# A hybrid decoder layer on one core: two instead of three of eight k-pairs by seven products, token sums formed with the tokens, and two of four weight sums formed by accumulating DMAs

## The chip, the cores and the metric

The kernel runs on one core of a Trainium2 chip. A time is the device time of one execution in microseconds (us). The kernel before takes 2048.77 us, the median of three runs (2047.95 to 2048.99). TensorE (PE) multiplies, VectorE (DVE) and ScalarE (ACT) do the elementwise work, SyncE (SP) issues loads and DMA transposes, GpSimd (POOL) does a few small operations.

## The reference

One decoder layer over 256 tokens of width 2048, in float32: a retention mixer and a gated linear recurrence side by side, merged by sigmoid gates, then cross-attention to 256 memory tokens, then a gated FFN. Nearly all of the time is products of the 256 tokens with weight matrices:

```python
ret_out = jax.nn.silu(g_ret) * ret
rnn_out = jax.nn.gelu(yr) * hr
merged = (jax.nn.sigmoid(g_a) * (ret_out @ w_proj_ret[l])
          + jax.nn.sigmoid(g_b) * (rnn_out @ w_proj_rnn[l]))
h = h + merged @ w_mix_out[l]
...
h = h + memory_cross_attention(hn, mem_n, xa_w_q[l], xa_w_k[l], xa_w_v[l], xa_w_o[l])
...
h = h + conv_gated_ffn(hn, ffn_w_up[l], ffn_conv_w[l], ffn_conv_b[l], ffn_w_down[l])
```

`g_a` and `g_b` are column ranges of `hn @ w_in`.

## The kernel before

**Three products for one.** Every float32 operand is split into a high part, rounded to float32r, and a low part, the rest. A product of two blocks is then three matmuls: high by high, low by high, high by low. ACT copies the high part of a weight (lines 326 and 339), DVE subtracts it to get the low part (328 and 340). The stationary operand is a 128 x 128 block of tokens, the moving one a 128 x 512 block of weights.

**Chunks.** `weight_plan` lists the matrix products in order, and `weights_in_order` lays all weights out in the order of their use, in chunks of 1 MB: 128 partitions x 4 blocks x 512 columns. `prefetch` loads a chunk into one of three `raw` buffers and splits it into `hi` and `lo` tiles (`PART_BUFS = 6` tiles of two blocks each); it keeps two chunks ahead of PE. `gemm_n` multiplies by one column block of 512; its chunk is four k-tiles, 24 matmuls.

**Pairs.** `steps_pair` multiplies by two column blocks at once. Its chunk is one k-pair (two k-tiles of 128) by both column blocks, and there are eight k-pairs to 2048 inputs. An ordinary k-pair takes 8 block products, 24 matmuls. A k-pair listed in `SEVEN` takes seven block products instead (Winograd's form of Strassen's scheme over two token tiles, two k-tiles and two column blocks), 21 matmuls. For it, `seven_parts` forms four sums of weight blocks on DVE (line 349) and splits seven blocks, and `sums_of` forms four sums of token blocks (lines 428 to 438: tiles `g`, `tq`, and `ts` for the split sums). `sums_of` is called from `steps_pair` one or two chunks ahead of the k-pair. The seven products are taken in the order p1, x3, p2, x5, p7, p6, p4; x3 is the first that reads `ts` and goes to a PSUM tile `sm`, so the profile shows it as `sm<-hi,ts`.

**Order of the stages.** Projections of `w_in` come first, then these pairs of column blocks, two per matrix: `w_proj_rnn`, gate columns `O_GA`, `w_proj_ret`, `w_mix_out`. A pair's eight chunks take some 41 us. After `w_proj_ret` the gates are applied (lines 934 and 956) and the rows are transposed by DMA (`by_dma`: ACT copies to `pl`, SP transposes into `pt`, ACT joins into `f`), and `turn_merged` splits them into the tokens of `w_mix_out`. Then come cross-attention (its `xa_w_o` has one pair, with `SEVEN_O`), and the FFN, whose first two `ffn_w_down` groups are two pairs each.

**Queues.** Each engine runs its instructions in the order in which they were recorded and scheduled; a waiting instruction holds what stands behind it. All loads and transposes stand in SP's one queue. At the start of `w_mix_out`, 4 MB of `x` and `mem` rows (tiles `nat`) are loaded through it too.

Of the kernel before, what the change touches and what calls it, by code (L numbers as in the profile page):

```python
# [17 lines left out]
P = 128  # L18
# [14 lines left out]
PART_BUFS = 6  # L33
# [8 lines left out]
SEVEN = (1, 3, 5)  # L42
# [25 lines left out]
def weight_plan():  # L68
# [81 lines left out]
def hybrid_layer(  # L150
# [106 lines left out]
    def prefetch(n):  # L257
        while len(ahead) < n and taken[0] < len(stream):
# [33 lines left out]
            own = early and i % 2 == 0  # L292
            cuts = () if i == 0 else range(0, nk + 1, KH) if i < 6 else (0, nk)
# [18 lines left out]
            if isinstance(c, tuple) and c[2]:  # L312
                ahead.append(((row, c), seven_parts(raw)))
                continue
            parts = []
            for k in range(0, nk, KH):
                if own:
                    xs[k2 + k // KH]
                hi = wp.tile([P, KH, BW], F32R, tag="hi", bufs=PART_BUFS, name=nm("hi"))
                lo = wp.tile([P, KH, BW], F32R, tag="lo", bufs=PART_BUFS, name=nm("lo"))  # L320
                for cs in (slice(k, k + 1), slice(k + 1, k + 2)) if i < 4 else (slice(k, k + KH),):
                    ds = slice(cs.start - k, cs.stop - k)
                    if i == 0 and cs.start == 0:
                        dve.tensor_copy(hi[:, ds], raw[:, cs, :])
                    else:
                        act.copy(hi[:, ds], raw[:, cs, :])  # L326
                    with tc.issue_after(split[cs.start]) if i == 0 else nullcontext():
                        dve.tensor_tensor(  # L328
                            out=lo[:, ds], in0=raw[:, cs, :], in1=hi[:, ds].bitcast(F32), op=ALU.subtract
                        )  # L330
                parts.append((hi, lo))
            ahead.append(((row, c), parts))

    def weight_parts(src):

        n = src.shape[1]
        hi = wp.tile([P, KH, BW], F32R, tag="hi", bufs=PART_BUFS, name=nm("hi"))
        lo = wp.tile([P, KH, BW], F32R, tag="lo", bufs=PART_BUFS, name=nm("lo"))
        act.copy(hi[:, 0:n], src)  # L339
        dve.tensor_tensor(out=lo[:, 0:n], in0=src, in1=hi[:, 0:n].bitcast(F32), op=ALU.subtract)  # L340
        return [(hi[:, i, :], lo[:, i, :]) for i in range(n)]

    def seven_parts(raw):

        b12, b11, b22, b21 = (raw[:, i, :] for i in range(4))
        p1, p3 = weight_parts(raw[:, 1:3])
        (p2,) = weight_parts(raw[:, 3:4])
        for o, a, b in ((b11, b12, b11), (b12, b12, b22), (b22, b11, b22), (b21, b22, b21)):
            dve.tensor_tensor(out=o, in0=a, in1=b, op=ALU.add)  # L349
# [42 lines left out]
    def steps_n(w, row, st, nk, col):  # L392
# [3 lines left out]
        for k0, n, parts in chunks(nk, w, row, col):  # L396

            def tile_(tt, kk):
                k = k0 + kk
                hi, lo = (t[:, kk % KH, :] for t in parts[kk // KH])  # L400
# [20 lines left out]
    def sums_of(t):  # L421

        if id(t) not in token_sums:
            g = big([P, 2, 2, P], s="g")
            o = big([P, 2, 4, P], F32R, s="ts")
            s = tmp("tq").rearrange("p a (b n) -> p (a b) n", b=2)
            flat = g.rearrange("p j i n -> p j (i n)")
            dve.tensor_tensor(
                out=flat, in0=t[:, :, 0:S].bitcast(F32), in1=t[:, :, S:BW].bitcast(F32), op=ALU.add
            )  # L430
            (a11, a21), (a12, a22) = ([g[:, j, i, :] for i in range(2)] for j in range(2))
            for d, a, b, op in (
                (0, a21, a22, ALU.subtract), (2, a11, a21, ALU.subtract),
                (1, s[:, 0, :], a11, ALU.subtract), (3, a12, s[:, 1, :], ALU.add),
            ):
                dve.tensor_tensor(out=s[:, d, :], in0=a, in1=b, op=op)
            act.copy(o[:, 0], s)  # L437
            dve.tensor_tensor(out=o[:, 1], in0=s, in1=o[:, 0].bitcast(F32), op=ALU.subtract)
            token_sums[id(t)] = (t, o)
        return token_sums[id(t)][1]  # L440

    def steps_pair(w, row, st, nk, c1, c2, seven=SEVEN):
# [14 lines left out]
        for k0, n, parts in chunks(nk, w, row, (c1, c2, seven)):  # L457
            k2 = k0 // KH
            for i in seven:
                if k2 < i <= k2 + 2:  # L460
                    sums_of(st[i])
# [5 lines left out]
            if k2 in seven:  # L467
# [5 lines left out]
                s1, s2, s3, s4 = ((ts[:, 0, i, :], ts[:, 1, i, :]) for i in range(4))  # L473
# [14 lines left out]
            else:  # L488
                end = k0 + n == nk
                for b, names in enumerate((("p2", "p4"), ("x3", "n"))):  # L490
                    hi, lo = parts[b]
# [219 lines left out]
    def split_head(h):  # L711
        f = words[h // 2][:, 2 * (h % 2) : 2 * (h % 2) + 2, :]
        ret.append(split_cols(f, lambda j: half_gn[:, 2 * h + j : 2 * h + j + 1]))

# [165 lines left out]
    for b in range(4):  # L880
# [28 lines left out]
        def gelu_y(f, xr=xr):  # L909
# [8 lines left out]
            for pr in range(2):  # L918
# [3 lines left out]
                rnn.append(split_pair(o, 0.5))  # L922
# [41 lines left out]
    def residual(w, st, out, wcol, steps=None):  # L964
# [3 lines left out]
        for b in range(4):  # L968
            if steps:
                steps(b)  # L970
            if not sources:
                if b == 0 or steps:
                    sources += pair(w, 0, st, NT, b * BW, (b + 1) * BW, *(() if steps else (SEVEN_O,)))
# [70 lines left out]
    def split_block(f):  # L1044
        return [split_pair(f[:, 2 * pr : 2 * pr + 2, :]) for pr in range(2)]
# [213 lines left out]
```

## Time and profile before

| what | number |
|---|---|
| median of three runs | 2048.77 us |
| the profiled execution's own time | 2047.84 us |
| its span, first to last instruction | 2046.1 us |
| mean granted TensorE clock | 0.987 |
| PE busy | 1991.3 us (97%), 8840 matmuls |
| DVE busy | 1542.0 us (75%) |
| ACT busy | 1343.0 us (66%) |
| POOL busy | 25.3 us (1%) |
| DMA | 425.60 MB, 208 GB/s mean |

The span is 1.7 us under the execution's time. Busy times are averages over stages with different limits: the pairs are read apart from the rest below. A matmul's duration in the rows (389 ns) overlaps with the next one's, so pace is read from counts in a stretch, not from durations.

### The profile page before, as it was taken

How to read it: one execution, taken by the hardware profiler on the slowest of the kernel's cores; microseconds unless marked ns; L12 is line 12 of the kernel's file. 1: busy time of each engine (PE TensorE's matmuls, PEld its weight loads, DVE VectorE, ACT ScalarE, POOL GpSimd, SP SyncE). 2: the span in 40 equal slices, each digit the busy share in tenths (PEclk: the TensorE clock that was granted, in tenths of full speed). 3: DMA queues.
4: the chain of work that ended last, by engine and by line, in shares of the span. 5: the costliest groups of instructions: out<-in, count | busy, mean ns of one | idle time of the engine just before them, and what ended most of it. 6: DMA issues, size and time to landing. Idle time of an engine off the chain costs nothing.

```text
span 2046.1 us, 23900 instructions
## 1 busy us (share of the span) xinstructions
PE 1991.3 (97%) x8840; PEld 1643.7 (80%) x8840; DVE 1542.0 (75%) x2029; ACT 1343.0 (66%) x1615; POOL 25.3 (1%) x25
## 2 busy tenths in 40 slices
PE   9999999999999999699999999999989999899998
PEld 8888888888887877577888888888877888788887
DVE  6857766998699999787555568666789676897675
ACT  7647548988454656678666667777765567654773
POOL 0000001000000000000000000000000000000000
PEclk9999999999999999799999999999999999999999
DMA  8755656665555556567766656767655677556773
GB/s 324 249 198 183 227 185 208 205 234 196 185 193 191 190 212 202 199 205 242 228 203 206 208 185 216 227 197 224 226 157 197 211 215 226 187 183 220 226 226 124
DMA packets 197188, 425.60 MB, mean 208 GB/s; under 512 B 142032, under 2 KB 146640, under 8 KB 152016
## 3 DMA queue, kind: packets, MB, share of 16 engines
q1 hardware_dynamic: 197072, 424.09, 62.8%
q8 instruction: 69, 1.13, 0.2%
q14 instruction: 47, 0.39, 0.1%
HBM read 388.39 MB, written 2.10 MB: 191 GB/s over the span
## 4 chain that ended last, share of the span: by engine, by line
PE 80%; DVE 9%; ACT 5%; issue 3%; DMA 2%; POOL 0%; POOLq 0%; SPq 0%; DVEq 0%; ACTq 0%
PE acc L235 72%; PE sm L235 8%; DVE lo L340 3%; DVE raw L349 2%; DVE lo L328 2%; ACT hi L326 1%; ACT f L533 1%; ACT hi L339 1%; DMA pt<-pl 1%; DMA raw<-in_wall 1%; ACT pl L520 1%; ACT s L579 0%; DMA nat<-in_mem 0%; DVE s L580 0%; DVE fv L1090 0%
## 5 line engine op out<-in xcount | busy, mean ns | idle before, releaser
L235 PE MATMUL acc<-hi,s 128*128 128x512 f32 (+1 forms) x4812 | 1481.4, 389 | 1.8 <-ACT hi L326 0.8
L235 PEld LDWEIGHTS acc<-hi,s 128*128 128x128 f32 x4812 | 903.3, 188 | 189.3 <-ACT s L579 1.5
L328 DVE TENSOR_TENSOR lo<-raw,hi 128x1024 fp32r<-128x1024 f32 (+1 forms) x640 | 770.8, 1224 | 358.0 <-ACT hi L326 349.4
L235 PE MATMUL acc<-lo,s 128*128 128x512 f32 (+1 forms) x2406 | 935.8, 389 | 2.4 <-DVE lo L340 1.8
L326 ACT CAST hi<-raw 128x1024 fp32r<-128x1024 f32 (+1 forms) x639 | 651.0, 1044 | 270.4 <-PE acc L235 189.5
L235 PEld LDWEIGHTS acc<-lo,s 128*128 128x128 f32 x2406 | 453.3, 188 | 97.9 <-DVE lo L340 3.2
L339 ACT CAST hi<-raw 128x1024 fp32r<-128x1024 f32 (+1 forms) x152 | 140.9, 942 | 166.5 <-DVE raw L349 111.5
L533 ACT COPY f<-pt 128x1024 uint16<-128x1024 uint16 x128 | 168.4, 1353 | 74.7 <-DMA pt<-pl 74.6
L340 DVE TENSOR_TENSOR lo<-raw,hi 128x1024 fp32r<-128x1024 f32 (+1 forms) x152 | 162.5, 1087 | 26.7 <-ACT hi L339 25.4
L235 PE MATMUL sm<-hi,s 128*128 128x512 f32 x528 | 162.6, 389 | 0.6 <-ACT hi L326 0.6
L520 ACT COPY pl<-rows 128x1024 uint16<-128x1024 uint16 x100 | 99.6, 1043 | 53.2 <-DVE rows L546 40.2
L235 PEld LDWEIGHTS sm<-hi,s 128*128 128x128 f32 x528 | 99.0, 188 | 21.4 <-ACT hi L326 1.0
L349 DVE TENSOR_TENSOR raw<-raw 128x512 f32<-128x512 f32 x152 | 104.4, 687 | 1.5
L235 PE MATMUL sm<-lo,s 128*128 128x512 f32 x264 | 102.8, 389 | 0.5 <-DVE lo L328 0.5
L235 PE MATMUL acc<-hi,ts 128*128 128x512 f32 x228 | 77.2, 423 | 3.5 <-ACT hi L339 3.4
L235 PE MATMUL sm<-hi,ts 128*128 128x512 f32 x76 | 28.6, 441 | 34.8 <-ACT ts L437 29.4
L235 PEld LDWEIGHTS acc<-hi,ts 128*128 128x128 f32 x228 | 47.0, 208 | 15.2 <-ACT hi L339 4.9
L235 PEld LDWEIGHTS sm<-lo,s 128*128 128x128 f32 x264 | 49.6, 188 | 11.3 <-DVE lo L328 1.0
L546 DVE TENSOR_SCALAR rows<-acc,ro 128x512 f32<-128x512 f32 x76 | 53.3, 744 | 4.2 <-PE acc L235 4.2
L1090 DVE SCALAR_TENSOR_TENSOR fg<-f,pf,fg 128x255 f32<-128x255 f32 (+1 forms) x88 | 37.6, 478 | 22.3 <-ACT fg L1088 22.0
L235 PEld LDWEIGHTS sm<-hi,ts 128*128 128x128 f32 x76 | 15.0, 197 | 43.4 <-ACT ts L437 32.3
L235 PE MATMUL acc<-lo,ts 128*128 128x512 f32 x114 | 47.5, 417 | 2.1 <-DVE lo L340 2.1
(179 smaller groups left out, 1008.6 us busy)
## 6 DMA issues: line engine op xcount, KB each, us to landing
raw<-in_wall SPq DMA_DIRECT2D x352, 1024.0 KB, 4.8
nat<-in_x SPq DMA_DIRECT2D x8, 512.0 KB, 9.3
raw<-in_wall SPq DMA_DIRECT2D x7, 512.0 KB, 5.7
pt<-pl SPq DMA_TRANSPOSE x128, 3.2
nat<-in_mem SPq DMA_DIRECT2D x4, 512.0 KB, 9.7
xt<-in_x_t SPq DMA_DIRECT2D x3, 512.0 KB, 9.1
xt<-in_mem_t SPq DMA_DIRECT2D x3, 512.0 KB, 7.0
dec<-in_consts SPq DMA_DIRECT2D x2, 512.0 KB, 4.3
```

Of the source, the lines that this page charges most:

```text
L235: tc.keep_in_program_order(pe.matmul(*a, **k))
L326: act.copy(hi[:, ds], raw[:, cs, :])
L328: dve.tensor_tensor(out=lo[:, ds], in0=raw[:, cs, :], in1=hi[:, ds].bitcast(F32), op=ALU.subtract)
L339: act.copy(hi[:, 0:n], src)
L340: dve.tensor_tensor(out=lo[:, 0:n], in0=src, in1=hi[:, 0:n].bitcast(F32), op=ALU.subtract)
L349: dve.tensor_tensor(out=o, in0=a, in1=b, op=ALU.add)
L520: act.copy(planes[:, tt], words[:, tt])
L533: act.copy(halves_[:, :, :, cs], turned_[:, :, :, cs])
L546: dve.tensor_scalar_mul(rows[:, tt, :], a[:, tt, :], r[:, tt : tt + 1])
L1090: dve.scalar_tensor_tensor(out=y[:, s:S], in0=z[:, j, 0 : S - s], scalar=pf[:, 2 - s, t : t + 1], in1=y[:, s:S], op0=ALU.mult, op1=ALU.add,)
```

## The change

- **Which k-pairs.** `SEVEN` goes from (1, 3, 5) to (2, 5); `SEVEN_O` stays (3, 5). The second half of `w_mix_out` becomes two ordinary column blocks, one after the other. Chunks by seven products go from 38 to 24.
- **Weight sums.** A seven chunk is no longer one load. SP loads its fourth block twice into `raw[:, 0:2]` (a broadcast read), its first block into a tile `b11` of the `tmp` pool, and its middle blocks into `raw[:, 2:4]`. Then GpSimd issues a DMA that adds blocks 0 and 1 from HBM onto `raw[:, 0:2]`. That forms two of the four sums; DVE forms the other two from them.
- **Part tiles.** `PART_BUFS = 6` tiles of two blocks become 3 tiles of four blocks. An ordinary chunk of a pair is split by one ACT copy and one DVE subtraction of 2048 columns instead of two of 1024; chunks of `gemm_n` keep two of each. A seven chunk takes two tiles.
- **Token sums.** `with_sums` forms the sums right after the split of the tokens that need them, from the unsplit source, with three DVE sums instead of five. For `w_in` and `ret` tokens the source is still added up first; `ret` sums are formed in `split_head`, `O_GA` sums up to three chunks ahead.

```diff
-PART_BUFS = 6
+PART_BUFS = 3
...
-SEVEN = (1, 3, 5)
+SEVEN = (2, 5)
 SEVEN_O = (3, 5)
...
-    for w, c in (("w_proj_rnn", 0), ("w_in", O_GA), ("w_proj_ret", 0), ("w_mix_out", 0)):
+    for w, c in (("w_proj_rnn", 0), ("w_in", O_GA), ("w_proj_ret", 0)):
         plan += [(w, 0, NT, (c + b * BW, c + (b + 1) * BW, SEVEN)) for b in (0, 2)]
+    plan += [("w_mix_out", 0, NT, (0, BW, SEVEN))] + [("w_mix_out", 0, NT, b * BW) for b in (2, 3)]
...
-        order = (b[:, 0], a[:, 0], b[:, 1], a[:, 1]) if c[2] else (a[:, 0], a[:, 1], b[:, 0], b[:, 1])
+        order = (a[:, 0], b[:, 1], a[:, 1], b[:, 0]) if c[2] else (a[:, 0], a[:, 1], b[:, 0], b[:, 1])
...
+            if seven:
+                b11 = tmp("b11").rearrange("p a n -> p (a n)")
+                load(raw[:, 0:2], src[:, 3:4, :].to_broadcast([P, KH, BW]), False)
+                load(b11, src[:, 0, :], False)
+                load(raw[:, 2:4], src[:, 1:3, :], False)
+                pool.dma_start(out=raw[:, 0:2], in_=src[:, 0:2, :], accum_op=ALU.add)
+                ahead.append(((row, c), seven_parts(raw, b11)))
+                continue
...
-        b12, b11, b22, b21 = (raw[:, i, :] for i in range(4))
-        p1, p3 = weight_parts(raw[:, 1:3])
-        (p2,) = weight_parts(raw[:, 3:4])
-        for o, a, b in ((b11, b12, b11), (b12, b12, b22), (b22, b11, b22), (b21, b22, b21)):
-            dve.tensor_tensor(out=o, in0=a, in1=b, op=ALU.add)
-        q3, q1 = weight_parts(raw[:, 0:2])
-        q2, q4 = weight_parts(raw[:, 2:4])
+        t1, t3, b22, b21 = (raw[:, i, :] for i in range(4))
+        p_hi, p_lo = part_tiles()
+        q_hi, q_lo = part_tiles()
+        weight_parts(b11, p_hi[:, 0, :], p_lo[:, 0, :])
+        weight_parts(raw[:, 2:4], p_hi[:, 1:3], p_lo[:, 1:3])
+        dve.tensor_tensor(out=b22, in0=t1, in1=b22, op=ALU.add)
+        dve.tensor_tensor(out=b21, in0=b22, in1=b21, op=ALU.add)
+        for c in (slice(0, 2), slice(2, 4)):
+            weight_parts(raw[:, c], q_hi[:, c], q_lo[:, c])
...
+    def with_sums(out, seven, src, scale=None):
+
+        t = split_pair(src, scale)
+        if len(out) in seven:
+            sums_of(t, src, scale)
+        out.append(t)
...
-                if k2 < i <= k2 + 2:
+                if k2 < i <= k2 + 3 and (not isinstance(st, list) or i < len(st)):
                     sums_of(st[i])
...
-            merged.append(split_pair(f[:, 2 * pr : 2 * pr + 2, :], 0.5))
+            with_sums(merged, SEVEN, f[:, 2 * pr : 2 * pr + 2, :], 0.5)
```

`rnn`, `osp` and `hid` tokens get `with_sums` in the same way as `merged`.

Three places show what moves. The first is DVE at the passage from the second pair of `w_proj_ret` to the first pair of `w_mix_out`; `raw_6650` is a seven chunk, L934 and L956 apply the gates, L328 splits an ordinary chunk, `g`, `tq` and `ts` are token sums. Before:

```order
L349 TENSOR_TENSOR raw_6650<-raw_6650 128x512
L934 TENSOR_SCALAR o_6610<-o_5912,o_6610 128x1024
L340 TENSOR_TENSOR lo_6669<-raw_6650,hi_6668 128x1024
L956 TENSOR_TENSOR o_6610<-o_6610,o_5206 128x1024
L328 TENSOR_TENSOR lo_6740<-raw_6737,hi_6739 128x1024
L328 TENSOR_TENSOR lo_6744<-raw_6737,hi_6743 128x1024
L428 TENSOR_TENSOR g_6747<-s_6455 128x512
L436 TENSOR_TENSOR tq_6749<-g_6747 128x128 x2
L436 TENSOR_TENSOR tq_6749<-tq_6749,g_6747 128x128
L436 TENSOR_TENSOR tq_6749<-g_6747,tq_6749 128x128
L428 TENSOR_TENSOR g_6804<-s_6464 128x512
L438 TENSOR_TENSOR ts_6748<-tq_6749,ts_6748 128x512
```

The same passage after the change; `raw_6274` is the first seven chunk of `w_mix_out`, `b_902_6275` its tile `b11`, and L980 applies a gate:

```order
L980 TENSOR_TENSOR o_6167<-o_6167,o_4928 128x1024
L347 TENSOR_TENSOR lo_6281<-b_902_6275,hi_6280 128x512
L347 TENSOR_TENSOR lo_6281<-raw_6274,hi_6280 128x1024
L356 TENSOR_TENSOR raw_6274<-raw_6274 128x512
L357 TENSOR_TENSOR raw_6274<-raw_6274 128x512
L347 TENSOR_TENSOR lo_6283<-raw_6274,hi_6282 128x1024 x2
L347 TENSOR_TENSOR lo_6322<-raw_6319,hi_6321 128x2048
L347 TENSOR_TENSOR lo_6369<-raw_6366,hi_6368 128x2048
L443 TENSOR_TENSOR tq_6359<-f_6349 128x256
```

The token sums of the first seven chunk no longer stand behind the gates (they were formed in the pair ahead), two weight sums stand where four stood, and the ordinary chunks behind are split by one row of 2048 columns each. `tq_6359` belongs to the second seven chunk of this pair.

The second place is SP's queue in the same passage, after the change (`raw_6274` as above, `raw_6405` and `b_924_6406` of the second seven chunk):

```order
L207 DMA raw_6274<-in_wall 128x2x512
L207 DMA raw_6274<-in_wall 128x1024
L207 DMA raw_6319<-in_wall 128x2048
L207 DMA raw_6366<-in_wall 128x2048
L543 DMA_TRANSPOSE pt_6240<-pl_6239 128x8x128 x2
...
L203 DMA nat_6259<-in_x 128x2x512
L207 DMA nat_6261<-in_mem 128x1024
...
L207 DMA nat_6267<-in_mem 128x1024
L207 DMA raw_6405<-in_wall 128x2x512
L207 DMA b_924_6406<-in_wall 128x512
L207 DMA raw_6405<-in_wall 128x1024
```

Where one load of 128x2048 stood for a seven chunk there are now three (that of `b11` may stand far ahead of the others), and those of the second seven chunk stand behind the eight `nat` loads, as its one load did before.

The third place is POOL from its last copies for the recurrence to the root of the memory norm, after the change:

```order
L867 TENSOR_TENSOR rp_3584<-rgw_3418,rp_3583 128x1024
L300 DMA raw_4443<-in_wall 128x1024
L300 DMA raw_4546<-in_wall 128x1024
...
L300 DMA raw_6274<-in_wall 128x1024
L300 DMA raw_6405<-in_wall 128x1024
L647 TENSOR_TENSOR ro_6484<-rv_6482,mhalf 128x2
```

Before, L842/L843 and L625 stood next to each other there. Fourteen accumulating DMAs now stand between them (ten more follow in later stages), each behind a wait for the broadcast load of its chunk.

More of the change, by code (lines that the diff above doesn't have):

```diff
@@ L311, in prefetch @@
                     sum_squares(xin[b], ss0, b)
[L312 to L315, printed above, removed]
+            hi, lo = part_tiles()
             for k in range(0, nk, KH):
@@ L330, in prefetch @@
                         )
[L331 to L341, printed above, removed]
@@ L1207, in hybrid_layer @@
             vl = big([P, 4, S], s="fv")
-            conv_up(FF, b, vl, lambda b=b, vl=vl: gate_up(gts[b], vl, hid.setdefault(b, [])))
+            b0 = max(one[1] for one in ff_plan() if one[0] == "down" and one[1] <= b)
+            seven = tuple(i - 2 * (b - b0) for i in SEVEN) if b0 < sum(FF_PARTS[:2]) else ()
+            conv_up(FF, b, vl, lambda b=b, vl=vl, n=seven: gate_up(gts[b], vl, hid.setdefault(b, []), n))
         else:
```

93 lines of the change are left out of this document (56 added, 37 removed).

## The prediction

> **What bounds the kernel now.** The page comes first: PE is busy 97% of the span.
>
> ```profile
> PE 1991.3 (97%) x8840; PEld 1643.7 (80%) x8840; DVE 1542.0 (75%) x2029; ACT 1343.0 (66%) x1615; POOL 25.3 (1%) x25
> ```
>
> That is an average. The chain of work that ended last, taken over the gate-and-value stage of the FFN, shows PE's undisturbed pace: 976 matmuls in 221.06 us, 0.2265 us each.
>
> ```profile
> 1263.12 221.06 PE acc L235 x976
> ```
>
> With that pace I read the busy time by stretches, one stretch for each pair of column blocks and one for the start of each `ffn_w_down` group. Behind the length stand PE's busy time and, in brackets, its matmuls; the last three columns are granted clock, DMA share and GB/s.
>
> ```profile
> 557.50:598.00 40.50, 40.50 (x181) 33.53 (x180) 39.93 (x58) 22.81 (x26) 0.00 (x0) 1.00 0.56 208
> 598.00:646.00 48.00, 45.86 (x203) 37.65 (x201) 45.87 (x52) 23.93 (x26) 0.00 (x0) 1.00 0.52 192
> 646.00:690.00 44.00, 42.25 (x178) 34.63 (x179) 41.38 (x64) 29.44 (x44) 0.00 (x0) 0.96 0.48 173
> 732.00:778.00 46.00, 44.08 (x193) 35.97 (x192) 44.17 (x60) 24.62 (x28) 0.00 (x0) 1.00 0.55 198
> 778.00:822.00 44.00, 41.38 (x178) 32.65 (x176) 39.92 (x48) 29.18 (x34) 0.00 (x0) 1.00 0.63 200
> 822.00:882.00 60.00, 44.47 (x152) 33.06 (x151) 44.58 (x64) 35.60 (x45) 0.70 (x1) 0.80 0.65 223
> 882.00:944.00 62.00, 57.57 (x239) 45.77 (x237) 52.19 (x67) 47.86 (x69) 0.00 (x0) 0.94 0.66 212
> 1496.00:1560.00 64.00, 55.47 (x234) 44.59 (x233) 62.39 (x95) 38.04 (x46) 0.00 (x0) 0.95 0.46 156
> 1762.00:1830.00 68.00, 61.45 (x257) 49.67 (x256) 66.16 (x98) 41.03 (x51) 0.00 (x0) 0.95 0.45 157
> ```
>
> Length less matmuls times 0.2265 is what PE lost. The first row lost nothing (181 matmuls are 41.0 us, the edges take half a microsecond). The others lost 2.0, 3.7, 2.3, 3.7, 25.6, 7.9, 11.0 and 9.8 us, **66 us** in all. DVE is busy over 90% in most of these rows, 39.93 of 40.50 us in the one without loss. So DVE is nearly as full as PE in the pairs, and whatever comes late on it stops PE. The waits of PE name it:
>
> ```profile
> PE sm L235 <- ACT ts L437: 29.4, 7, 9.2
> PE sm L235 <- DVE ts L438: 5.4, 6, 1.1
> ```
>
> 34.8 us are waits for token sums. The longest stands in the timeline of PE at the first seven chunk of `w_mix_out`; DVE's timeline shows that the sum it needs began at 829.01, behind the split of a later chunk:
>
> ```profile
> 831.46 1.52 PE L235 MATMUL sm<-hi,ts 128*128 128x512 f32 x2 [9.21 <-ACT ts L437]
> ```
> ```profile
> 826.74 2.35 DVE L328 TENSOR_TENSOR lo<-raw,hi 128x1024 fp32r<-128x1024 f32 x2
> 829.01 0.69 DVE L428 TENSOR_TENSOR g<-s 128x512 f32<-128x512 f32 x1
> ```
>
> The rest of the 66 us is the slow clock behind such gaps (0.80 in 822 to 882) and small waits for weight parts.
>
> **The change part by part.** All sums are against the profiled execution, 2047.84 us, whose span is 2046.1 us; it lies 0.9 us under the median of the runs.
>
> *Fewer seven chunks.* 38 become 24, and each of the 14 needs 3 matmuls more: 42 x 0.2265 = **+9.5 us**, certain, since PE is on the path there.
>
> *DVE and ACT per pair.* The groups by line and form:
>
> ```profile
> L328 DVE TENSOR_TENSOR lo<-raw,hi 128x1024 fp32r<-128x1024 f32 x632 | 765.6, 1231 | 357.1 <-ACT hi L326 348.4 <-PE acc L235 0.9 <-PE sm L235 0.4
> L340 DVE TENSOR_TENSOR lo<-raw,hi 128x1024 fp32r<-128x1024 f32 x114 | 138.9, 1221 | 26.6 <-ACT hi L339 25.4
> L349 DVE TENSOR_TENSOR raw<-raw 128x512 f32<-128x512 f32 x152 | 104.4, 687 | 1.5
> L340 DVE TENSOR_TENSOR lo<-raw,hi 128x512 fp32r<-128x512 f32 x38 | 26.0, 685 | 0.1
> L339 ACT CAST hi<-raw 128x1024 fp32r<-128x1024 f32 x114 | 119.7, 1051 | 158.0 <-DVE raw L349 111.5 <-PE acc L235 22.2 <-PE sm L235 13.4
> L339 ACT CAST hi<-raw 128x512 fp32r<-128x512 f32 x38 | 23.5, 617 | 8.5 <-PE sm L235 8.2 <-PE acc L235 0.3
> L428 DVE TENSOR_TENSOR g<-s 128x512 f32<-128x512 f32 x20 | 13.7, 685 | 0.0
> ```
>
> A seven chunk costs DVE 3 x 1.221 + 0.685 + 4 x 0.687 = 7.1 us before and, with two sums, 5.7 us after. An ordinary chunk is 2 x 1.231 = 2.46 us; by the line through 685 and 1221 ns one of 2048 columns takes 2.29 us (ACT 1.92), an estimate. A pair has 3 seven and 5 ordinary chunks before: 33.6 us of DVE beside 183 matmuls, 41.4 us. After, 2 and 6: 25.2 us beside 186 matmuls, 42.1 us. So 8.4 us of DVE go from each pair, 100 us over twelve pairs. Token sums are formed for two k-pairs of a stage instead of three, without line 428 where the source is given. DVE goes from full to some four fifths, so its backlog ends.
>
> *The stalls.* The first k-pair that needs token sums is now the third, not the second, and its sums stand with the split, a pair earlier. I take away most of each loss. Of 11.7 us in the four small rows 2.5 stay. In `ffn_w_down` (20.8) 4 stay: the burst of convolutions and gates ahead of it still meets the first chunks. The second half of `w_mix_out` (7.9) becomes ordinary blocks, of the kind that lost nothing in the FFN: 0 stay. In its first half (25.6) 8 stay. There ACT waits for 4 MB of rows, and the loads of the second seven chunk stand behind these in SP's queue (the order above):
>
> ```profile
> 841.78 1.06 ACT L608 ACTIVATE nat<-nat 128x1024 f32<-128x1024 f32 x1 [10.38 <-DMA nat<-in_mem]
> ```
> ```profile
> raw<-in_wall SPq DMA_DIRECT2D x16, 1024.0 KB, 4.7
> q1 hardware_dynamic: 2304, 16.78, 53.9%
> ```
> ```profile
> nat<-in_mem SPq DMA_DIRECT2D x4, 512.0 KB, 9.7
> ```
>
> The two middle rows are loads and queue of 557 to 640: 16 MB kept the engines busy for 0.539 x 83 = 44.7 us, 2.8 us a megabyte, so the 4 MB take 11 us. I put their start 9 us behind the pair's first matmul (four gate rows of 1024 columns at 1.22, then copies and transposes, an estimate); 11 us of loads, then 10.1 for the chain of the next load and its accumulate and 4.9 for sums and split (both worked out below) end at 35 us. PE wants the first sum after two ordinary chunks, a seven, two ordinary and nine products, 10.9 + 4.8 + 10.9 + 2.0 = 28.6 us. That is 6 us, and 2 more for the rows ACT waits for. Sum of the stalls: 66 - 14.5 = **-51.5 us**. Bounds: all 66 go, or only the 34.8 us of direct waits less the same remainder (-20).
>
> A word on the clock in what stays. By the row of 822 to 882 PE idled 15.5 us (60 less 44.47) and lost 25.6, so 10 us were slow matmuls. The Trainium skill ("TensorE: Matmul & The Clock Gate", Part 1) has the clock halved only after an idle window of about 3.4 us; by that rule, if what stays there is made of shorter waits, 5 us and not 8 stay and the sum is 3 us less; by the row's own ratio it is 8, which I keep.
>
> *Coarser part tiles.* Three tiles of four blocks. A seven chunk holds two, so the ordinary chunk behind it can be split only once PE has ended the chunk before the seven one. Its split is one ACT copy and one DVE subtraction in turn, 1.92 + 2.29 = 4.2 us; the seven chunk covers 21 x 0.2265 = 4.8, and the low part is first read by the third matmul, 0.45 later. That leaves 1.0 us. Any instruction of 1 to 2.4 us that ACT or DVE is in the midst of eats it. Lower bound 0; upper bound one such instruction on each, less the slack, 1.2 + 1.2 - 1.0 = 1.4 us in each of 24 places, 34 us. I take 0.25 us each, **+6 us**, near the lower end, since DVE then has a fifth of its time free. In stages of `gemm_n` the halves stay and two chunks of 24 matmuls cover the split: nothing.
>
> *The accumulating DMA.* No row shows one. It moves 512 KB in and reads 512 KB back: the nearest row is the load of 1 MB at 4.7 us, of which 2.8 is transfer. Lower bound 1.9 + 1.4 = 3.3 us; upper bound twice a 512 KB load in the fullest queue, 2 x 9.7 = 19.4 us. I take 4.7. Ahead of it lies the broadcast load, 3.3 us, and beside it 768 KB of the other two, 2.1 us: 10.1 us from the free buffer to the sums. What covers it: the buffer of the second seven chunk is free about when PE starts the first one, or 1.8 us sooner (split in 2 x 1.22 + 1.05 = 3.5 us after a tile came free 5.4 us earlier). Three chunks (4.8 + 5.4 + 5.4) and nine products (2.0) later PE reads its first sum, and the two DVE sums and the split need 1.4 + 3.5 us ahead. 1.8 + 17.6 - 4.9 = 14.5 us of cover: **0 us**, with 4.4 us to spare, so an accumulate may take 9.1 us before PE waits. GpSimd's own share is behind no one: its next work is the small root of a norm. Should the DVE sum wait, behind it stand the splits of the same and the next chunks, which PE needs last. For the price alone: the Trainium skill ("DMA: Bandwidth & Descriptors", "Anatomy of one DMA") gives a GpSimd DMA 2.0 us plus its bytes at 436 GB/s, an estimate of 3.2 us for 512 KB; the sum would be the same.
>
> *Loads.* 24 chunks write 1.75 MB instead of 1. In a pair that is 9.5 MB instead of 8; at 2.8 us a megabyte 27 us of 42: hidden.
>
> Sum: 2047.8 + 9.5 - 51.5 + 6.0 = 2011.8, on the scale of the runs **2012 us**.
>
> **The rivals.** *A, all stalls go and nothing new comes:* 2047.8 + 9.5 - 66 = 1991 us. For it: the stretch 557 to 598 kept pace with DVE at 99%. Against: the `nat` loads stay where they were.
>
> *B, the coarse tiles eat the gain:* the place behind each seven chunk costs its upper bound, 34 us in place of 6: 2040 us. Against: DVE's free fifth. For: before, halves came free half a chunk sooner, and this is the only cover that shrinks in every pair.
>
> *C, slower: the accumulate lands late.* It decides from 9.1 us on; 36 us of gain are gone at 1.5 us per seven chunk, 10.6 us to landing, about the 9.7 us row. At 12 us each of 24 chunks loses 2.9 us: 2012 + 70 = 2082 us. For it: the engines have to read, add and write back, and 9.7 us was seen for 512 KB. Against: that was behind 4 MB; the queue of the pairs is at 0.46 to 0.66.
>
> *D, the change does not do what it says:* the order shows the sums and the DMAs moved as stated, and a scheduler that keeps the stalls in place would give 2047.8 + 9.5 = 2057 us.
>
> **How the numbers follow.** Forecast (2000 to 2025) 52%, A and what lies under 2000 15%, B (2025 to 2044) 16%, C 13%, D 4%. C and D are slower, 17%; of the rest some 3% lie within 0.2% of the time before (4 us, about what a measurement of this kernel can tell from no change), 80% faster. The range leaves out the lower part of A (4%) and the far part of C and D (14%): 1988 to 2054 us.
>
> **What would show it.** Right: the waits of PE for `ts` under 5 us (34.8 before), DVE at least 100 us less busy (1542 before), PE with 8882 matmuls, the stretch of the first `w_mix_out` pair short of 52 us. The accumulate's row of issues shows a landing of 4 to 9 us, and DVE's sums (line 356) wait for it little. B would show as waits of PE `acc` or `sm` for `lo` and `hi` of line 346 and 347 just behind seven chunks. C would show as DVE waiting at line 356 for the DMA, 24 times, and PE behind. The forecast is wrong if the token sums were only the last of several late things on DVE, so that PE's waits move to another name and keep their length.

## The result, and the profile after

The changed kernel takes 2023.3 us, the median of four runs (2020.9 to 2027.2), beside 2048.4 us for the kernel before. The ratio is 0.988, with a 95% interval from 0.9863 to 0.9897: 25 us less, where 36 were forecast. The profiled execution took 2027.23 us, 3.9 us over its own median, with a span of 2025.5 us.

The page of after, first part, and GpSimd's DMA queue (packets, MB, share):

```profile
PE 1990.3 (98%) x8882; PEld 1648.0 (81%) x8882; DVE 1418.7 (70%) x1757; ACT 1296.5 (64%) x1508; POOL 46.3 (2%) x49
...
q0 software_dynamic: 3456, 12.58, 3.6%
```

PE has the 42 matmuls more, DVE is 123 us less busy, ACT 46 us, and a second queue has appeared: 24 accumulating DMAs of 512 KB. Now the waits of PE in the changed kernel (in total, times, longest):

```profile
PE acc L236 <- DVE lo L347: 7.1, 8, 1.7
PE acc L236 <- ACT s L578: 6.2, 1, 6.2
PE acc L236 <- ACT hi L346: 5.6, 2, 3.3
PE sm L236 <- ACT ti L883: 4.5, 1, 4.5
PE acc L236 <- ACT hi L334: 1.9, 1, 1.9
```

No wait for `ts` is left (34.8 us before). What stands there instead are weight parts (`lo`, `hi`), token parts (`s`) and, at `ti`, the scan of the recurrence, a stage that the change was not thought to touch.

The stretches of after, with the columns of the prediction's windows, show where. The first is the part before the pairs; then come the pairs up to `w_mix_out`, its first half, its second half, and the two `ffn_w_down` groups:

```profile
20.00:540.00 520.00, 512.90 (x2348) 427.33 (x2348) 380.43 (x527) 355.41 (x443) 19.82 (x11) 0.99 0.64 215
540.00:820.00 280.00, 272.94 (x1185) 223.52 (x1184) 204.99 (x208) 147.06 (x140) 10.64 (x12) 0.99 0.70 222
820.00:880.00 60.00, 48.14 (x185) 37.06 (x184) 39.33 (x42) 35.01 (x38) 2.46 (x3) 0.87 0.79 256
880.00:1000.00 120.00, 120.00 (x528) 99.35 (x527) 77.07 (x97) 87.64 (x119) 0.70 (x1) 0.99 0.73 236
1490.00:1600.00 110.00, 109.59 (x484) 90.46 (x483) 84.55 (x87) 56.37 (x52) 3.54 (x4) 1.00 0.66 219
1750.00:1860.00 110.00, 109.64 (x484) 90.47 (x483) 83.64 (x84) 55.67 (x53) 3.48 (x4) 1.00 0.68 219
```

and the kernel before, in the first of them:

```profile
20.00:540.00 520.00, 519.81 (x2395) 434.22 (x2394) 387.08 (x524) 362.91 (x448) 19.75 (x11) 1.00 0.65 216
```

From 880 on PE is busy almost without a break: the second half of `w_mix_out` and both FFN groups keep pace. But 820 to 880 still holds only 185 matmuls, one pair, in 60 us, and the first 520 us, where the kernel before lost nothing, now hold 47 matmuls less.

To put one number on each stretch I summed, over all matmuls of a trace, by how much the distance from one start to the next exceeds the pace (0.2267 us for 512 columns, 0.12 for 256). Slow matmuls behind a gap count in it, and a wait counts in the stretch in which it ends. The stage names are those of the changed kernel; in the kernels that lost less ahead of it, `w_mix_out` begins up to some 20 us sooner. The first two columns are the kernels before and after; the other three are the experiments that matter most, told below.

| stretch (us) | before | after | two_only | two_early | no_accum |
|---|---|---|---|---|---|
| 20 to 540, retention and recurrence | 0.5 | 11.0 | 0.6 | 5.8 | 11.7 |
| 540 to 780, first pairs | 8.5 | 3.4 | 0 | 0 | 0 |
| 780 to 820, end of the last `w_proj_ret` pair | 3.9 | 8.4 | 0 | 0 | 3.2 |
| 820 to 880, first half of `w_mix_out` | 26.0 | 18.2 | 18.9 | 14.3 | 13.7 |
| 880 to 1000 | 11.5 | 1.2 | 0 | 0 | 0 |
| both `ffn_w_down` groups | 21.6 | 1.4 | 7.9 | 0.8 | 1.3 |
| whole execution | 75.9 | 45.9 | 32.1 | 23.4 | 32.9 |

75.9 to 45.9 is 30 us gained; less 9.5 us of matmuls, that is 20.5, and the two spans differ by 20.6. So the table holds the whole difference of the two profiled executions. It also gives the question: 46 us are left where the forecast, 14.5 + 6 and the few us of the start, expected some 23.

### The profile page after: what moved, and what is told of

The parts are those of the page before. It is cut to its first block, busy times and chain, and to the rows that moved or that the text cites. A ratio compares the mean times of both kernels' runs of the same rounds, so it can differ in the third digit from the quotient of the medians.

```text
span 2025.5 us, 23201 instructions
## 1 busy us (share of the span) xinstructions
PE 1990.3 (98%) x8882; PEld 1648.0 (81%) x8882; DVE 1418.7 (70%) x1757; ACT 1296.5 (64%) x1508; POOL 46.3 (2%) x49
## 4 chain that ended last, share of the span: by engine, by line
PE 85%; DMA 5%; DVE 5%; ACT 3%; issue 2%; POOL 0%; SPq 0%; POOLq 0%; DVEq 0%; ACTq 0%
PE acc L236 76%; PE sm L236 9%; DMA raw<-in_wall 3%; DVE lo L347 1%; DVE lo L336 1%; DMA pt<-pl 1%; ACT pl L542 1%; ACT hi L346 1%; DMA b<-in_wall 0%; ACT hi L334 0%; DVE xr L918 0%; ACT f L555 0%; DMA nat<-in_x 0%; DVE fg L1116 0%; DVE raw L356 0%
## 5 line engine op out<-in xcount | busy, mean ns | idle before, releaser
L236 PE MATMUL acc<-hi,s 128*128 128x512 f32 x4904 | 1509.9, 389 | 10.4 <-ACT s L578 6.2
L236 PE MATMUL acc<-lo,s 128*128 128x512 f32 x2452 | 954.7, 389 | 4.6 <-DVE lo L347 3.9
L336 DVE TENSOR_TENSOR lo<-raw,hi 128x1024 fp32r<-128x1024 f32 (+1 forms) x524 | 621.1, 1216 | 285.3 <-ACT hi L334 284.7
L334 ACT CAST hi<-raw 128x1024 fp32r<-128x1024 f32 (+1 forms) x523 | 522.1, 1042 | 346.6 <-PE acc L236 231.5
L347 DVE TENSOR_TENSOR lo<-raw,hi 128x2048 fp32r<-128x2048 f32 (+1 forms) x144 | 250.3, 1755 | 103.2 <-ACT hi L346 102.7
L346 ACT CAST hi<-raw 128x2048 fp32r<-128x2048 f32 (+1 forms) x144 | 211.3, 1480 | 160.0 <-PE sm L236 88.4
L542 ACT COPY pl<-rows 128x1024 uint16<-128x1024 uint16 x100 | 99.4, 1043 | 17.8 <-DVE rows L566 9.0
L1116 DVE SCALAR_TENSOR_TENSOR fv<-f,pf,fv 128x255 f32<-128x255 f32 (+1 forms) x88 | 37.6, 480 | 19.8 <-ACT fv L1114 19.4
L1116 DVE SCALAR_TENSOR_TENSOR fg<-f,pf,fg 128x255 f32<-128x255 f32 (+1 forms) x88 | 37.6, 480 | 17.8 <-ACT fg L1114 17.4
L236 PE MATMUL acc<-hi,ts 128*128 128x512 f32 x144 | 46.1, 402 | 3.3 <-ACT hi L346 3.3
L300 POOL DMA_DIRECT2D raw<-in_wall x24 | 21.2, 883 | 1178.2 <-DMA raw<-in_wall 663.4
L236 PEld LDWEIGHTS acc<-hi,ts 128*128 128x128 f32 x144 | 28.0, 195 | 9.6 <-ACT hi L346 3.8
```

The lines of the kernel that those rows point to most:

```text
L236: tc.keep_in_program_order(pe.matmul(*a, **k))
L300: pool.dma_start(out=raw[:, 0:2], in_=src[:, 0:2, :], accum_op=ALU.add)
L334: act.copy(hi[:, cs], raw[:, cs, :])
L336: dve.tensor_tensor(out=lo[:, cs], in0=raw[:, cs, :], in1=hi[:, cs].bitcast(F32), op=ALU.subtract)
L346: act.copy(hi, src)
L347: dve.tensor_tensor(out=lo, in0=src, in1=hi.bitcast(F32), op=ALU.subtract)
```

## The experiments

Each was timed in four runs against the kernel before on the same chip (medians 2049.9 to 2050.5 us). Ratios have 95% intervals of about 0.0016 to either side, 3 us, so two versions differ for certain from 4 to 5 us on. All of them compute the whole layer.

**two_only: the choice of k-pairs alone.** From the kernel before:

```diff
-SEVEN = (1, 3, 5)
+SEVEN = (2, 5)
...
-    for w, c in (("w_proj_rnn", 0), ("w_in", O_GA), ("w_proj_ret", 0), ("w_mix_out", 0)):
+    for w, c in (("w_proj_rnn", 0), ("w_in", O_GA), ("w_proj_ret", 0)):
...
+    plan += [("w_mix_out", 0, NT, (0, BW, SEVEN))] + [("w_mix_out", 0, NT, b * BW) for b in (2, 3)]
```

> The kernel before with only the choice of k-pairs changed: two of eight by seven products, the second half of w_mix_out as two ordinary blocks. Four DVE sums per seven chunk, token sums on demand and tiles of two blocks stay. Theory 1 (DVE's backlog is the cause, and any part that takes work from DVE removes most of it): DVE falls to 2 x 7.1 + 6 x 2.46 = 29 us of 42 per pair, 42 matmuls more (+9.5), 45 of 66 us of stalls go: 2013 us. Theory 2 (the token sums' place is the cause, not the load): the sums still stand behind the backlog of the gates, 10 to 20 us go: 2038 to 2048 us.

2012.27 us, ratio 0.9813 (0.9797 to 0.983): 38 us gained, more than by the whole change. The waits of PE for token sums in it:

```profile
PE sm L236 <- ACT ts L438: 13.2, 4, 6.4
PE sm L236 <- DVE ts L439: 3.8, 5, 1.1
```

Half of the 34.8 us stay, since the sums are still made on demand. The rest of the change therefore costs 13 us on balance, though it removes these waits.

**two_at_1: the same with other k-pairs.** From `two_only`:

```diff
-SEVEN = (2, 5)
+SEVEN = (1, 4)
```

> The run with the choice of pairs alone, with (1, 4) in place of (2, 5): as many seven chunks and as little work for DVE, but the first one is again the second chunk of a pair. Load theory (less work on DVE ends the backlog, the place matters little): 2010 to 2018 us. Place theory (the sums need two chunks of lead over the gates' and the convolutions' bursts): waits for ts come back at the first chunks of w_mix_out and of both ffn_w_down groups, 15 to 25 us: 2028 to 2038 us.

2025.95 us, ratio 0.9885 (0.9869 to 0.9902), between the two theories. Against before, 24 us come from having less for DVE to do (with a plain second half of `w_mix_out`, which this run doesn't tell apart); against `two_only`, 15 us hang on where the two seven chunks stand. The place shows at the first of them:

```profile
821.64 1.52 PE L236 MATMUL sm<-hi,ts 128*128 128x512 f32 x2 [6.24 <-ACT ts L438]
```

**coarse_only: three tiles of four blocks alone.** From the kernel before:

```diff
-PART_BUFS = 6
+PART_BUFS = 3
...
+                if isinstance(c, tuple):
+                    if k == 0:
+                        weight_parts(raw, hi, lo)
+                    continue
```

> The kernel before with only the part tiles changed: three of four blocks, whole splits in the ordinary chunks of a pair. Theory 1 (the coarse tiles cost what ACT and DVE are in the midst of): with DVE full in the pairs and 38 places behind a seven chunk, 0.5 to 1 us each, plus stalls in the retention and recurrence stages at 330 and 438 us as in the changed kernel (8 to 11 us): 2070 to 2095 us. Rival (the coarse tiles are free; the stalls at 330 and 438 come from the token sums made there): 2046 to 2052 us.

2079.87 us, ratio 1.0148 (1.0132 to 1.0163): 30 us slower. The waits of PE in it; the lines are shifted by one or two against the kernel before:

```profile
PE acc L235 <- DVE lo L340: 15.8, 13, 1.8
...
PE acc L235 <- ACT hi L339: 8.8, 4, 5.3
PE sm L235 <- ACT ti L862: 3.7, 2, 1.9
```

In this kernel L339 and L340 split every chunk of a pair, the ordinary ones too, so their 24.6 us stand beside all waits for weight parts before (L339 and L340 with L326 and L328), 9.7 us. The waits for `ti` grow from 0.2 us. By the sum of the table 9.2 us are lost before 540 us, in stages without any pair (0.5 before the change). That leaves some 21 of the 30 us for the pairs and 38 seven chunks, 0.55 us for each, even with DVE as full as it was; the prediction's upper bound had 1.4 us.

**two_early: early token sums, without coarse tiles and accumulates.** `two_only` with `with_sums` and the shorter `sums_of` of the change, six tiles of two blocks, one load and four DVE sums for a seven chunk:

```diff
+    def with_sums(out, seven, src, scale=None):
+
+        t = split_pair(src, scale)
+        if len(out) in seven:
+            sums_of(t, src, scale)
+        out.append(t)
```

> The kernel before with the choice of k-pairs and the early token sums: four DVE sums of weights, six tiles of two blocks. Theory 1 (with fine tiles the sums' place is worth the waits for ts that the run with the choice of pairs alone still has in the two ffn_w_down groups and at the first w_mix_out pair, 3 + 5 + some of 13 us): 2001 to 2007 us. Rival (the place of the sums is worth nothing, as in the changed kernel): 2010 to 2015 us.

2004.43 us, ratio 0.9775 (0.976 to 0.9789), 46 us under before. Against `two_only` it saves 7.1 us in `ffn_w_down` and 4.6 in the first half of `w_mix_out`, and pays 5.2 us before 540: ACT waits there for a token sum that is wanted much later, and the recurrence's `ti` stands behind it in ACT's queue. ACT in this kernel, 6 us ahead of a gap of 1.2 us on PE that ends with `ti`:

```profile
430.86 0.64 ACT L443 ACTIVATE ts<-tq 128x512 fp32r<-128x512 f32 x1 [2.35 <-DVE tq L438]
```

**no_accum: the change without its accumulating DMAs.** From after:

```diff
-                load(raw[:, 0:2], src[:, 3:4, :].to_broadcast([P, KH, BW]), False)
-                load(b11, src[:, 0, :], False)
-                load(raw[:, 2:4], src[:, 1:3, :], False)
-                pool.dma_start(out=raw[:, 0:2], in_=src[:, 0:2, :], accum_op=ALU.add)
+                load(raw, src, False)
...
-        dve.tensor_tensor(out=b22, in0=t1, in1=b22, op=ALU.add)
-        dve.tensor_tensor(out=b21, in0=b22, in1=b21, op=ALU.add)
+        for o, a, b in ((b11, b12, b11), (b12, b12, b22), (b22, b11, b22), (b21, b22, b21)):
+            dve.tensor_tensor(out=o, in0=a, in1=b, op=ALU.add)
```

> The changed kernel with one load per seven chunk and all four weight sums on DVE; pairs, tiles and token sums as changed. Theory 1 (DVE has room once only two k-pairs are left, and the accumulate's chain of loads is itself late in places): DVE gains 24 x 1.37 = 33 us of work, hidden, and the waits for b11 and the accumulate (8 to 13 us at 720, 807 and 870) go: 2008 to 2018 us. Rival (taking two sums off DVE is what made the gain): 2035 us or more.

2013.87 us, ratio 0.9823 (0.9808 to 0.9838). The accumulates save DVE 31 us (1450.2 against 1418.7 busy) and cost 9 us by the medians, 12 by the ratios. The table says where: all of it between 700 and 880. Of `two_early` this kernel is the version with coarse tiles, and 9 to 10 us slower; two thirds of that lie before 540.

**after_fine: the change with six tiles of two blocks.** From after:

```diff
-PART_BUFS = 3
+PART_BUFS = 6
...
-        p_hi, p_lo = part_tiles()
-        q_hi, q_lo = part_tiles()
+        (p1,) = weight_parts(b11[:, None, :])
+        p3, p2 = weight_parts(raw[:, 2:4])
```

> The changed kernel with the part tiles of before: six of two blocks, splits of 1024 columns; accumulating DMAs, early token sums and choice of pairs as changed. Theory 1 (the coarse tiles cost 10 us between 20 and 540 us and 3 to 5 us in the pairs): 2008 to 2013 us, and no stall over 1 us before 540 us. Rival (the early token sums and the DMAs, not the tiles, make the early stalls): 2019 to 2025 us.

2017.37 us, ratio 0.9843 (0.9826 to 0.986): 6 us of the coarse tiles come back by the medians, 8 by the ratios, between what the two theories had. The gap at 333 us is gone, and the loss before 540 falls from 11.0 to 4.1 us; two waits for `ti`, 1.5 us each, stay, much as in `two_early`, and so do the accumulates. 820 to 880 loses 17.8 us, as much as after: PE's wait for `s` there is 9.0 us instead of 6.2.

**halves: coarse tiles, but a chunk of a pair split in two steps.** From after:

```diff
-                        weight_parts(raw, hi, lo)
+                        for cs in (slice(0, KH), slice(KH, KC)):
+                            weight_parts(raw[:, cs], hi[:, cs], lo[:, cs])
```

> The changed kernel with the ordinary chunks of a pair split in two halves of 1024 columns again, into the same three tiles of four blocks. If the length of one split (1.92 + 2.29 us in turn) is what the coarse tiles cost in the pairs: 2016 to 2020 us. If it is the tile, which comes free only as a whole, and the stages of single blocks, whose splits were halves already: 2021 to 2026 us, and the stalls before 540 us stay at 10 to 12 us.

2019.65 us, ratio 0.9849 (0.9835 to 0.9864): 4 us under the change by the medians, 6 by the ratios, at the edge of what these runs can tell, and in the range of the first theory. The time from 540 to 820 loses 3.8 us instead of 11.8, with no wait of PE over 0.5 us, though the accumulates land no sooner (median 7.9 us beside 6.4). This speaks for the length of a split counting where loads come late. How much of the 8 us is that, and how much the timing of the loads, stays open: `after_fine`, with halves too, loses 9.1 us there. The loss before 540 is 11.9 us, as in after; this run can't show a cause there, since its edit changes nothing ahead of the pairs. The split there is in halves in before, after and `after_fine` alike, so what differs between these is the tile.

**late_sums: the change with token sums on demand.** From after:

```diff
-        if len(out) in seven:
-            sums_of(t, src, scale)
...
-                if k2 < i <= k2 + 3 and (not isinstance(st, list) or i < len(st)):
+                if k2 < i <= k2 + 2 and (not isinstance(st, list) or i < len(st)):
```

> The changed kernel with the token sums on demand again, one or two chunks ahead, from the split tokens (five DVE sums as three, line 437 back). Theory 1 (load on DVE): the sums find a DVE with room and cost little: 2023 to 2032 us. Theory 2 (their place): waits for ts come back at the first seven chunk of w_mix_out and of each ffn_w_down group, 15 to 25 us: 2038 to 2048 us.

2020.7 us, ratio 0.9856 (0.984 to 0.9871). As a whole the sums on demand cost nothing, a little less than the first theory had. The second theory's waits come back at one of its three places, the first half of `w_mix_out`:

```profile
PE sm L236 <- ACT ts L447: 8.7, 2, 5.8
```

There they take the place of other waits: that for `s` falls from 6.2 to 1.1 us, and the stretch loses 16.0 us, after 18.2. `ffn_w_down` loses 0.8 us. Besides the add of line 437 this version keeps the short form of `sums_of`, three DVE sums. So of the 8 us between `two_only` and `two_early` it stays open what comes from the earlier place and what from fewer instructions.

**b11_own: own buffers for `b11`.** From after (and one buffer less in the pool `bp`, for room):

```diff
-                b11 = tmp("b11").rearrange("p a n -> p (a n)")
+                b11 = wp.tile([P, BW], F32, tag="b11", bufs=B11_BUFS, name=nm("b11"))
```

> The changed kernel with two buffers of their own for b11 in place of the shared temporaries (and 28 big buffers instead of 29, to make room). If b11's load waits for a temporary and so stands behind two later loads in SP's queue (the 4 us wait for b11 at 805): the 8 us lost at 780 to 820 fall to 3, 2015 to 2020 us. Rival (the loads are late by their number and size): 2021 to 2026 us.

2020.28 us, ratio 0.9855 (0.984 to 0.987), between the two theories. The wait for `b11` goes and 780 to 820 loses 4.6 us instead of 8.4. But `halves`, which keeps the shared buffers, loses 3.2 us there, so it isn't shown that the buffers make the difference. And a wait for `raw` stands in place of that for `b11`:

```profile
ACT hi L347 <- DMA raw<-in_wall: 4.3, 1, 4.3
```

**The rows of memory, three runs.** At the start of `w_mix_out` ACT waits for `nat` rows. `mem_late` (from after) and `two_early_mem` (from `two_early`) move the memory's loads and sums of squares to the third block of `w_mix_out`; `two_early_sq` moves only the sums of squares, by this edit (the other two also move the loads, with `mnat.extend(load_half(mem, i) for i in range(4))` at the new place):

```diff
     def memory_steps(b):
-        if b == 0:
+        if b == 2:
+            ms.load(2)
             ss = sums()[:, :, 0:2]
```

> The changed kernel with the four loads of mem rows and their sums of squares moved from the start of w_mix_out to its third column block. Theory 1 (what is left at 820 to 880 us is ACT waiting for these rows and the second seven chunk's loads standing behind them): 12 to 16 of 18 us go, 2007 to 2012 us. Rival (the second seven chunk is late by its own chain of load and accumulate): the gap of 6 us at the join of the tokens goes, that at 870 us stays, 2015 to 2019 us.

> The choice of k-pairs, the early token sums and the late loads of mem rows; fine tiles, four DVE sums. Theory 1 (the parts add up): 2048 + 9.5 less some 63 of the 72 us of stalls, 1992 to 1998 us. Rival (the waits move to the x rows and the transposes behind them in SP's queue): 2003 to 2010 us.

> The choice of pairs and the early token sums, fine tiles, four DVE sums; the loads of mem rows stay where they were, and only their sums of squares on ACT go from the first block pair of w_mix_out to its third block. Theory 1 (ACT, waiting for rows that land late, holds the joins of the tokens behind it; moving the loads only moved that wait): the gap of 7 us at 833 and the slow clock behind it go, 1991 to 1997 us. Rival (the joins wait for the transposes themselves): 2001 to 2006 us.

2021.59 us (ratio 0.9865, 0.9845 to 0.9884), 2006.32 (0.9783, 0.9769 to 0.9798) and 2002.35 (0.9765, 0.9751 to 0.978). No first theory came true: `mem_late` gains nothing clear of noise, and the other two lie in their rivals' ranges. In `two_early_mem` 820 to 880 loses 5.7 us, down from 14.3, and 880 to 1000 loses 10.8, up from nothing: at their new place ACT waits 2.3 us for the rows and then works on them and on the next tokens for 19 us ahead of a copy of weights (`hi`), for which PE waits 7.3 us.

With the squares alone moved, PE's wait for `s` (6.8 us) goes, and a wait of 4.1 us for a copy of weights stands there. The rival's number came true and not its mechanism: the joins are done by 836, and ACT waits for a load. It is that of the second seven chunk, which stands behind the eight loads of rows in SP's queue, as the prediction had it; the three loads of 1 MB there take 12.9 us from issue to landing:

```profile
841.98 1.04 ACT L342 CAST hi<-raw 128x1024 fp32r<-128x1024 f32 x1 [5.97 <-DMA raw<-in_wall]
```

`two_early_sq` is the fastest version found, 2.35% under before and some 1% under the change; that it beats `two_early` is within the intervals.

## Why the prediction was right or wrong, step by step

The experiments lie on one path, so each term has a run of its own. Lost time is that of the table:

| term of the sum | forecast | measured | from |
|---|---|---|---|
| 42 matmuls more | +9.5 | +9.5 | 8882 counted, pace kept from 880 on |
| stalls that go | -51.5 | -52.5 | before 75.9, two_early 23.4 |
| coarser part tiles | +6 | +9.5 | two_early 23.4, no_accum 32.9 |
| accumulating DMAs | 0 | +13.0 | no_accum 32.9, after 45.9 |
| sum, profiled executions | -36 | -20.5 | spans 2046.1 and 2025.5 |

By the ratios of the timed runs the first two terms are together -46 us (`two_early`), the last two +10 and +12, and the sum -25; the profiled execution of after was the slowest of its four, which is why the table's 13.0 is high. Taken in the other order, with `after_fine` between, the ratios give 14 us for the accumulates and 8 for the tiles. So each is known to a few us.

**The accumulates at nothing: the step that failed.** The prediction took 4.7 us from issue to landing and said that PE is safe up to 9.1. The 24 issues of after:

```profile
L300 POOL DMA_DIRECT2D raw<-in_wall x24: 862/872/1064, 556.3 to 1815.1; - x24
...
  ACT hi L346: 19.8, 5
  DVE raw L356: 18.8, 7
DMA to landing us min/median/max: 5.3/6.4/11.0
```

The median, 6.4 us, is over the 4.7 taken and within the limit; the other price in the prediction, 3.2 us, lies under all 24. Three landings are over the limit (9.6, 9.9 and 11.0 us, all between 700 and 820). Rival C had 10.6 us at every chunk. The latest of them, at 706 us, in the rows of SP and GpSimd, then in the loads from 700 to 720 (count, KB each, median us to landing):

```profile
702.26 1.71 SPq L207 DMA_DIRECT2D raw<-in_wall  x2
704.03 0.43 SPq L207 DMA_DIRECT2D b<-in_wall  x1
706.78 2.87 SPq L207 DMA_DIRECT2D raw<-in_wall  x2
709.70 1.90 SPq L207 DMA_DIRECT2D b<-in_wall  x3
```
```profile
706.82 0.88 POOL L300 DMA_DIRECT2D raw<-in_wall  x1 [18.17 <-DVE lo L347]
```
```profile
raw<-in_wall SPq DMA_DIRECT2D x2, 1024.0 KB, 10.8
...
b<-in_wall SPq DMA_DIRECT2D x4, 256.0 KB, 10.9
raw<-in_wall POOLq DMA_DIRECT2D x1, 512.0 KB, 11.0
```

Within 10 us SP sends two halves and the `b` tile of the seven chunk, then two whole chunks and three `b` tiles for later chunks, and GpSimd sends its accumulate. The halves and the first `b` land after 4 to 6 us. What is issued from 706.8 us on, the whole chunks, three `b` tiles and the accumulate, all lands after some 11 us, 256 KB like 1 MB. The prediction had counted the bytes of a pair (27 us of 42) and called the loads hidden; their mean is, but the loads bunch. DVE then stands, with splits and a token sum behind it:

```profile
717.89 0.69 DVE L356 TENSOR_TENSOR raw<-raw 128x512 f32<-128x512 f32 x1 [6.21 <-DMA raw<-in_wall]
```
```profile
721.77 0.50 PE L236 MATMUL acc<-lo,ts 128*128 128x512 f32 x1 [1.72 <-DVE lo L347]
```

PE pays 1.7 us for 6.2 of DVE here, as the cover had it. Ahead of `w_mix_out` it pays more, and there it is the small load `b11`, a transfer that the four sums on DVE never needed, that holds ACT:

```profile
808.97 0.62 ACT L346 CAST hi<-b 128x512 fp32r<-128x512 f32 x1 [3.98 <-DMA b<-in_wall]
```

So C's mechanism is real at about a fifth of the 70 us that it was priced at, or less. What a late landing costs seems to hang also on what stands behind it: in `halves`, with shorter splits, PE waits little for landings just as late. That it is the bunching which makes these landings late is read from the traces alone; no run spread the loads.

**Coarse tiles: right in kind, mis-sized, and in the wrong place.** "In stages of `gemm_n` the halves stay and two chunks of 24 matmuls cover the split: nothing" fell. ACT in the kernel before, at 325 us:

```profile
324.98 1.98 ACT L520 COPY pl<-rows 128x1024 uint16<-128x1024 uint16 x2
326.86 2.00 ACT L326 CAST hi<-raw 128x1024 fp32r<-128x1024 f32 x2
328.76 1.71 ACT L770 ACTIVATE rows<-rc,ro 128x256 f32<-128x256 f32 x4
330.37 1.98 ACT L520 COPY pl<-rows 128x1024 uint16<-128x1024 uint16 x2
332.25 1.99 ACT L326 CAST hi<-raw 128x1024 fp32r<-128x1024 f32 x2
```

and after, with PE behind it:

```profile
324.63 1.98 ACT L542 COPY pl<-rows 128x1024 uint16<-128x1024 uint16 x2
326.51 1.70 ACT L794 ACTIVATE rows<-rc,ro 128x256 f32<-128x256 f32 x4
328.12 3.87 ACT L542 COPY pl<-rows 128x1024 uint16<-128x1024 uint16 x4
331.90 4.84 ACT L334 CAST hi<-raw 128x1024 fp32r<-128x1024 f32 x5
```
```profile
332.99 0.73 PE L236 MATMUL acc<-hi,s 128*128 128x512 f32 x2 [1.90 <-ACT hi L334]
```

Before, copies of weights stand between the row copies. After, ten other instructions go ahead of them: 7.4 us of row work in one piece, then five weight copies at once. A whole tile of four blocks comes free half a chunk, or 12 matmuls (2.7 us), later than one of two; that the order follows from this is read from the rows. That the tile is the cause is shown: coarse tiles add 6 to 9 us before 540 in `coarse_only` and `no_accum`, and with six tiles (`after_fine`) the order of before is back. The cover of two chunks was worked out for a free engine, not for ACT's queue in this stage. In the pairs some 4 of the 6 us came, with DVE's free fifth. Rival B's 34 us did not come even with a full DVE: `coarse_only` loses some 21 us in its pairs.

**The stalls: right as a sum, in part by luck.** The forecast took 51.5 of 66 us in its stretches. The 52.5 measured are of the whole execution: in the pairs and the FFN groups 56 us went, and the early sums brought 5.3 new ones before 540, where the forecast had nothing (1.4 went elsewhere). That the two sums agree to 1 us is luck; the parts do not. Token-sum waits are gone, `ffn_w_down` keeps 1.4 us where 4 were left, and the second half of `w_mix_out` keeps pace. Its first half kept 18.2 us, not 8 (14.3 without coarse tiles and accumulates). It was to be "short of 52 us"; it took 60. The mechanism was the one named, ACT behind the `nat` rows, but the price counted only the wait for loads. ACT after, and PE:

```profile
840.12 3.96 ACT L346 CAST hi<-raw 128x2048 fp32r<-128x2048 f32 x2 [0.51 <-ACT hi L346]
...
852.35 1.06 ACT L630 ACTIVATE nat<-nat 128x1024 f32<-128x1024 f32 x1 [8.27 <-DMA nat<-in_mem]
```
```profile
856.61 1.52 PE L236 MATMUL acc<-hi,s 128*128 128x512 f32 x2 [6.15 <-ACT s L578]
...
873.76 1.22 PE L236 MATMUL acc<-hi,ts 128*128 128x512 f32 x2 [3.34 <-ACT hi L346]
```

ACT waits 8.3 us for rows that no one needs yet; the joins of the next tokens stand behind it, and PE waits 6.2 us for these tokens. The second gap is that of the second seven chunk, whose loads stand behind the rows: 3.3 us, against 6 forecast. On the clock: in 820 to 880 PE idled 11.9 us and lost 18.2, so 6.3 us were slow matmuls (granted 0.87). The gap of 6.2 us is past the window of 3.4 us that the Trainium skill ("TensorE: Matmul & The Clock Gate", Part 1) gives, and behind it the clock fell, as by that rule. But in the same trace it fell behind a shorter gap too: PE waited 2.23 and then 0.66 us up to 811.0, and from 812 to 818 the granted clock was 0.57. Behind the wait of 1.72 us at 722 it stayed at 1.00 (718 to 724). So the prediction's second case, that shorter waits leave the clock alone, does not hold here for all of them.

**The signs.** No waits for `ts`, 123 us less of DVE and 8882 matmuls came as said. The first pair did not, nor did landings of 4 to 9 us in every place, and DVE's sums (line 356) waited 18.8 us for them, which is not little. Rival A's 1991 us was not reached; `two_early_sq` at 2002 shows that without coarse tiles and accumulates most of it is there. D is refuted.

**What stays open.** Whether the second seven chunk of `w_mix_out` would be in time if its load stood ahead of the loads of rows; how much of the 8 us between `two_only` and `two_early` is the place of the sums; what the accumulates would cost if the loads were spread, or with shorter splits; and how `b11_own` would do without giving up a buffer of `bp`.

## What to carry to other kernels

When a change consists of several parts, measure the part that cuts work alone: here choosing fewer seven chunks, at better places, gave 38 us and the early sums 8 more, while two parts that were meant to relieve DVE further gave back some 20, because DVE's load was no longer what PE waited for. Taking work from an engine that has time paid nothing here, and its price (a longer chain of transfers, a coarser buffer) was paid elsewhere. Price a buffer's size in every stage that uses it, and a landing by the loads issued next to it, not by the mean load of the queues.

## What the runs showed of the hardware

- An accumulating DMA of 512 KB from GpSimd landed in 5.3 to 11.0 us, median 6.4, beside 4.9 us for a plain load of 1 MB; it occupied GpSimd for 0.87 us.
- The granted clock was 0.57 over the 6 us behind waits of PE of 2.23 and 0.66 us with little work between them, and 1.00 behind a single wait of 1.72 us (both in after).
- A load of 256 KB took longer than one of 1 MB, 6.7 against 4.9 us, where it was issued among them:

```profile
raw<-in_wall SPq DMA_DIRECT2D x328, 1024.0 KB, 4.9
...
raw<-in_wall POOLq DMA_DIRECT2D x24, 512.0 KB, 6.4
b<-in_wall SPq DMA_DIRECT2D x24, 256.0 KB, 6.7
```

- The line through 685 and 1221 ns held out to 2048 columns: 2.29 us on DVE and 1.92 on ACT were estimated. Groups of after:

```profile
L347 DVE TENSOR_TENSOR lo<-raw,hi 128x2048 fp32r<-128x2048 f32 x72 | 163.5, 2289 | 82.8 <-ACT hi L346 82.6
L346 ACT CAST hi<-raw 128x2048 fp32r<-128x2048 f32 x72 | 137.2, 1911 | 86.4 <-PE sm L236 50.3 <-PE acc L236 14.0 <-issue 13.2
```
